# A fused two-block transformer layer on one core: the order of side work and the engine of each copy are read from two tables in the source instead of worked out while the program is built

## The chip, the core and the metric

The kernel runs on one core of a Trainium2 chip. A core has five engines that run their own instruction streams in order and meet at semaphores: TensorE (PE in the profile; its weight loads are listed apart as PEld), VectorE (DVE), ScalarE (ACT), GpSimd (POOL) and SyncE (SP), which here only issues DMAs. The metric is device microseconds of one execution: 865.17, the median of three (864.73 to 866.28).

## What is computed

The reference runs 256 tokens of width 1024, with 16 tokens put in front in the first block, through two blocks in fp32:

```python
# block 1
u = rmsnorm(h, g_pre_mix);  q, k, v, xr, yr = split(u @ w_in)
attn = sliding_window_attention_with_sinks(q, k, v, sinks)   # 8 heads of 64
hr   = rg_lru(causal_depthwise_conv(xr), w_a, b_a, w_x, b_x, lam)
mix  = concat([attn, gelu(yr) * hr]) @ w_out
h = h + rmsnorm(mix, g_post_mix)
h = h + rmsnorm(square(relu(rmsnorm(h, g_pre_ffn) @ w_ff1)) @ w_ff2, g_post_ffn)
# block 2 (after the 16 front tokens are cut off)
u = rms_norm(h, ln_pre_mix);  q_a, k_a, v_a, qkv_b, z_b, b_b, a_b, gate_a, gate_b = split(u @ w_in)
y_a = moba_attention(rope(q_a), rope(k_a), v_a)              # 8 heads of 128
y_b = rms_norm(gated_delta_rule(silu(conv(qkv_b)), decay(a_b), sigmoid(b_b))) * silu(z_b)
merged = sigmoid(gate_a) * (y_a @ w_proj_a) + sigmoid(gate_b) * (y_b @ w_proj_b)
h = h + rms_norm(merged @ w_out, ln_post_mix)
f = rms_norm(h, ln_pre_ffn)
h = h + rms_norm((silu(f @ w_ffn_gate) * (f @ w_ffn_up)) @ w_ffn_down, ln_post_ffn)
h = h + sigmoid(h @ w_ple_gate) * rms_norm(p @ w_ple, ln_ple)
```

## The kernel before

**Products.** Every large product is made in three passes on TensorE, because both factors are split into a hi and a lo part: `mm3` (line 192) issues hi x hi, hi x lo and lo x hi into one PSUM bank. The weights come as 258 tiles of 128x1024 fp32. A tile is loaded by one DMA into `raw` (4 buffers) and split in two halves of 512 columns by `hilo` (line 207): `copy` writes the hi half (`whi`), a VectorE subtraction writes the lo half (`wlo`). Nine pairs of `whi` and `wlo` are held. Activations are split in the same way where they are made (`uT`, `hm`, `mixT`, `yaT`, `mgT`).

**Main work and side work.** `run` (line 327) goes through a list of jobs, each a weight tile or two and its products. Between products a job calls `tick` (line 305). All that isn't a weight product stands in side streams, Python generators started by `side`: the attention of four head pairs (`attn`, line 718), the recurrence gates (`lru_gates`, `rec`), the layer boundaries (`chain_norm`, line 497), and in block 2 the gates, the MoBA attention (`moba2`), the convolved q, k, v (`qkv_post`, line 1086) and the gated delta rule of four head pairs (`gdn`, line 1146). A stream yields the tiles that it needs next. An engine runs its instructions in the order in which the program emits them, so `tick` sets the order on all engines.

**What sets the order.** While the program is built, every call of an engine goes through the class `Timed` (line 101 on), so all instructions of the profile carry its line, L111. It adds an estimated duration to a `Clock` of that engine. `tick` advances a stream when its tiles would be done by TensorE's estimated time, and `prefetch` (line 274) prepares half a weight when one of the next two weights lacks it, or when the estimates of ScalarE, VectorE and the DMA's arrival lie less than `AHEAD` past TensorE's:

```python
on_dve = start_of("dve", src) + (DCP if src.tensor.name in clk.bank else DHI)
if on_dve < start_of("act", src):
    dve.tensor_copy(dst, src)
else:
    act.activation(dst, src, AF.Copy)
...
while s in sides and clk.of(*s[0]) + HOP <= clk.now["pe"] + (LEAD if isinstance(s[0], Soon) else SLACK):
...
    pos["prep"] < pos["use"] + URGENT or
    max(clk.now["act"], clk.now["dve"], arrival()) < clk.now["pe"] + AHEAD):
```

**Names that come up later.** In block 1: `s_m` and `s_r` are the softmax maxima and sums, the copies `g<-ps` of 128x512 in `q_post` bring two query pairs out of PSUM, `mixT` is the split input of w_out, its last rows made by `rec` (line 821) from a GpSimd product. At a layer boundary `m` is the product with the gain, `ms` the mean square, raised to the power -1/2 by GpSimd, `h` the residual and `u` the normed tile, which TensorE transposes into `uT`. In block 2: `gm` is a GpSimd product of gates and a mask, which a TensorE product with `mgt` (line 1111) turns into the decay of a head pair. `A` in `gdn` is the scaled product of k with itself, multiplied with a mask on GpSimd; `cmp` is the sum over it, which goes through a scratch tensor `sc` in memory to 32 rows of `w`, on which GpSimd runs a recurrence of 28 small operations (`tmp`, `g`); `sk`, `rk`, `bk`, `nk` are scalars of the rows of k.

Of the kernel before, what the change touches and what calls it, by code (L numbers as in the profile page):

```python
# [53 lines left out]
SAME = dict(act=0.1, dve=0.12, pool=0.1, pe=0.0, dma=0.0)  # L54


class Clock:


    def __init__(self):  # L60
        self.now = dict.fromkeys(("act", "dve", "pool", "pe", "dma"), 0.0)
        self.done, self.read, self.by = {}, {}, {}
        self.bank, self.user = {}, {}

    def of(self, *tiles):
        return max((self.done.get(t.tensor.name, 0.0) for t in tiles), default=0.0)

    def step(self, eng, cost, outs, ins):
        t = self.now[eng]
        for n in ins:  # L70
            t = max(t, self.done.get(n, 0.0) + (HOP if self.by.get(n) != eng else SAME[eng]))
            if n in self.bank:
                t = max(t, self.bank[n] if self.user.get(n) != eng else 0.0)
        for n in outs:
            if n in self.bank:
                t = max(t, self.read.get(n, 0.0), self.done.get(n, 0.0) if self.by.get(n) != eng else 0.0)
        end = t + cost
        self.now[eng] = end - 2.0 if eng == "dma" else end
        for n in ins:
            self.read[n] = max(self.read.get(n, 0.0), end)  # L80
            if n in self.bank:
                self.bank[n], self.user[n] = end, eng
        for n in outs:
            self.done[n], self.by[n] = end, eng


class Soon(tuple):
    pass


def parts_of(x):

    n = x.tensor.name
    if not n.startswith("uT"):
        return [n]
    dims = [d[1] for d in x.ap[1:]]
    (k, c), m = divmod(x.offset, TM), dims[0] if len(dims) > 1 else 1
    return [f"{n}.{i}.{j}" for i in range(k // 4, (k + m - 1) // 4 + 1) for j in range(c // P, (c + dims[-1] - 1) // P + 1)]


class Timed:


    def __init__(self, clock, eng, name):
        self.clock, self.eng, self.name = clock, eng, name

    def __getattr__(self, op):
        call = getattr(self.eng, op)

        def f(*args, **kw):  # L110
            r = call(*args, **kw)  # L111
            aps = [(k, x) for k, x in list(enumerate(args)) + list(kw.items()) if hasattr(x, "tensor")]
            outs = [n for k, x in aps if k in (0, "out", "accum_out") for n in parts_of(x)]
            ins = [n for k, x in aps if k not in (0, "out", "accum_out") for n in parts_of(x)]
            o = args[0] if args else kw["out"]
            n = o.free_size()
            if "dma" in op:
                self.clock.step("dma", 2.0 + 3.1e-6 * n * o.partition_size() * 4, outs, ins)
                return r
            if self.name == "pe":  # L120
                if op == "transpose":
                    cost = 0.11
                elif kw["rhs"].dtype == F32R:
                    cost = max(0.104, 0.422e-3 * n)
                else:
                    cost = 1.69e-3 * max(n, kw["lhsT"].free_size())
            elif self.name == "act":
                extra = sum(hasattr(kw.get(k), "tensor") for k in ("accum_out", "scale", "bias"))
                cost = (0.051 if ins[0] in self.clock.bank else 0.093) + 0.833e-3 * n + 0.093 * extra
            elif self.name == "dve":  # L130
                m = max(x.free_size() for k, x in aps)
                cost = 0.07 + (0.52e-3 if op == "tensor_copy" and ins[0] not in self.clock.bank else 1.04e-3) * m
            elif kw.get("op") == ALU.pow:
                cost = 0.3 + 0.165 * n
            elif op == "tensor_scalar":
                cost = 0.175 + 3.33e-3 * n + 0.09 * (len(aps) - 2)
            else:
                cost = 0.15 + 2.1e-3 * n
            self.clock.step(self.name, cost, outs, ins)
            return r  # L140
        return f
# [3 lines left out]
def griffin_then_moba_gdn_kernel(ctx: ExitStack, tc, a, out):  # L145
    nc = tc.nc
    clk = Clock()
    act, dve, pool, pe, dma = (Timed(clk, e, n) for e, n in (
        (nc.scalar, "act"), (nc.vector, "dve"), (nc.gpsimd, "pool"), (nc.tensor, "pe"), (nc.sync, "dma")))
# [104 lines left out]
    def prep():  # L254
        i = pos["prep"]
        if not half:
            assert i < pos["free"] + NW
# [21 lines left out]

    def weight(j):  # L280
        i = pos["base"] + j
        pos["use"] = max(pos["use"], i + 1)
        while pos["prep"] <= i:
            prep()
        return wts[i]

    def free(j):
        pos["free"] = pos["base"] + j
        for i in [i for i in wts if i < pos["free"]]:
            del wts[i]  # L290
# [1222 lines left out]
```

## Time and profile before

| what | value |
|---|---|
| median of three runs | 865.17 us (864.73 to 866.28) |
| the profiled execution | 865.83 us, span 864.0 |
| TensorE busy | 848.0 us, 98% |
| VectorE busy | 620.3 us, 72% |
| ScalarE busy | 449.9 us, 52% |
| GpSimd busy | 160.0 us, 19% |
| DMA | 147.18 MB, 170 GB/s on the mean |

The span runs from the first to the last instruction that the profiler saw; 1.83 us of the profiled execution lie around it. Busy time counts instructions, so an engine can be busy and still run slower than it could (TensorE at a lower clock, VectorE beside GpSimd). A timeline row gives the start, the duration of all the instructions merged in it, the engine, the operation, output and inputs, the count, and in square brackets the idle time just before with what ended it.

### The profile page before, as it was taken

How to read it: one execution, taken by the hardware profiler on the slowest of the kernel's cores; microseconds unless marked ns; L12 is line 12 of the kernel's file. 1: busy time of each engine (PE TensorE's matmuls, PEld its weight loads, DVE VectorE, ACT ScalarE, POOL GpSimd, SP SyncE). 2: the span in 40 equal slices, each digit the busy share in tenths (PEclk: the TensorE clock that was granted, in tenths of full speed). 3: DMA queues.
4: the chain of work that ended last, by engine and by line, in shares of the span. 5: the costliest groups of instructions: out<-in, count | busy, mean ns of one | idle time of the engine just before them, and what ended most of it. 6: DMA issues, size and time to landing. Idle time of an engine off the chain costs nothing.

```text
span 864.0 us, 15454 instructions
## 1 busy us (share of the span) xinstructions
PE 848.0 (98%) x5905; PEld 777.2 (90%) x5905; DVE 620.3 (72%) x1135; ACT 449.9 (52%) x1004; POOL 160.0 (19%) x248
## 2 busy tenths in 40 slices
PE   9999999999999999999999999999999999999997
PEld 7988679999999789999989999999977999999987
DVE  6996887555555558988788899777857756655562
ACT  6756666554445454446644473455536544544441
POOL 3411100000000005220363568401300001000001
PEclk9999999999999999999999999999999999999999
DMA  7645537766566246234661345445636768565611
GB/s 260 235 122 178 196 109 262 242 193 195 194 186 186 68 131 235 84 116 145 210 213 50 102 153 184 153 144 181 196 129 183 236 211 277 184 197 179 192 50 50
DMA packets 47772, 147.18 MB, mean 170 GB/s; under 512 B 9281, under 2 KB 10561, under 8 KB 47698
## 3 DMA queue, kind: packets, MB, share of 16 engines
q1 hardware_dynamic: 47554, 146.13, 52.6%
q8 instruction: 46, 0.75, 0.4%
q14 instruction: 28, 0.23, 0.1%
q10 hardware_dynamic: 144, 0.07, 0.0%
HBM read 143.82 MB, written 2.36 MB: 169 GB/s over the span
## 4 chain that ended last, share of the span: by engine, by line
PE 80%; DVE 7%; POOL 5%; DMA 3%; ACT 3%; issue 2%; SPq 0%; POOLq 0%; ACTq 0%; DVEq 0%
PE ps L111 80%; POOL g L111 3%; DVE g L111 2%; DVE wlo L111 2%; POOL tmp L111 2%; ACT g L111 1%; ACT whi L111 1%; DVE s_m L111 1%; DMA raw<-in_w1in 1%; DMA raw<-in_ff1t 1%; DMA xmt<-in_meta 1%; DVE whi L111 0%; DMA gain<-in_rows 0%; DVE u L111 0%; POOL aq L111 0%
## 5 line engine op out<-in xcount | busy, mean ns | idle before, releaser
L111 PE MATMUL ps<-uT,whi 128*128 128x256 f32 (+1 forms) x2272 | 418.1, 285 | 0.0
L111 DVE TENSOR_TENSOR wlo<-raw,whi 128x512 fp32r<-128x512 f32 x513 | 349.4, 724 | 85.8 <-ACT whi L111 83.2
L111 PEld LDWEIGHTS ps<-uT,whi 128*128 128x128 f32 x2272 | 351.9, 189 | 4.5 <-issue 0.8
L111 ACT ACTIVATE whi<-raw 128x512 fp32r<-128x512 f32 x485 | 275.3, 622 | 101.3 <-issue 65.2
L111 PE MATMUL ps<-uT,wlo 128*128 128x256 f32 (+1 forms) x1136 | 319.5, 281 | 0.0
L111 PEld LDWEIGHTS ps<-uT,wlo 128*128 128x128 f32 x1136 | 215.4, 190 | 0.0
L111 PE MATMUL ps<-whi,hm 128*128 128x512 f32 x432 | 138.8, 393 | 0.0
L111 ACT ACTIVATE g<-ps 128x512 f32<-128x512 f32 (+4 forms) x104 | 51.4, 508 | 124.0 <-PE ps L111 122.0
L111 PEld LDWEIGHTS ps<-whi,hm 128*128 128x128 f32 x432 | 81.3, 188 | 17.6
L111 PE MATMUL ps<-wlo,hm 128*128 128x512 f32 x216 | 85.0, 394 | 0.0
L111 PE MATMUL ps<-whi,uT 128*128 128x512 f32 (+1 forms) x256 | 75.8, 376 | 1.0 <-ACT uT L111 0.7
L111 PE MATMUL ps<-g 128*128 128x128 f32 (+9 forms) x560 | 73.0, 278 | 3.1 <-ACT g L111 1.9
L111 POOL TENSOR_TENSOR ms<-ms,mhalf 128x1 f32<-128x1 f32 (+1 forms) x19 | 11.7, 615 | 347.4 <-DVE ms L111 347.3
L111 PEld LDWEIGHTS ps<-g 128*128 128x128 f32 (+5 forms) x560 | 62.6, 176 | 9.3 <-issue 3.1
L111 PEld LDWEIGHTS ps<-whi,uT 128*128 128x128 f32 x256 | 46.3, 191 | 12.2 <-DVE uT L111 2.4
L111 POOL TENSOR_TENSOR g<-g 128x512 f32<-128x512 f32 (+1 forms) x20 | 31.5, 1580 | 113.2 <-DVE g L111 91.9
L111 PEld LDWEIGHTS ps<-wlo,hm 128*128 128x128 f32 x216 | 40.6, 188 | 8.3
L111 PE MATMUL ps<-wlo,uT 128*128 128x512 f32 (+1 forms) x128 | 47.5, 371 | 0.0
L111 DVE SCALAR_TENSOR_TENSOR g<-ps,vec,g 128x255 f32<-128x255 f32 (+5 forms) x84 | 35.0, 475 | 2.7 <-ACT g L111 2.4
L111 ACT ACTIVATE junk<-ps 128x128 bf16<-128x128 f32 (+1 forms) x48 | 17.9, 382 | 30.1 <-PE ps L111 30.0
L111 ACT ACTIVATE hm<-g 128x512 fp32r<-128x512 f32 x23 | 14.5, 632 | 32.5 <-DVE g L111 32.5
L111 DVE SCALAR_TENSOR_TENSOR g<-g,ps 128x512 f32<-128x512 f32 x23 | 15.7, 681 | 17.3 <-ACT g L111 14.3
(166 smaller groups left out, 870.1 us busy)
## 6 DMA issues: line engine op xcount, KB each, us to landing
raw<-in_ff SPq DMA_DIRECT2D x60, 512.0 KB, 4.4
raw<-in_w2qkv SPq DMA_DIRECT2D x24, 512.0 KB, 3.8
raw<-in_ffdown SPq DMA_DIRECT2D x22, 512.0 KB, 4.4
raw<-in_ffg SPq DMA_DIRECT2D x18, 512.0 KB, 4.4
raw<-in_ffu SPq DMA_DIRECT2D x18, 512.0 KB, 4.0
raw<-in_w1in SPq DMA_DIRECT2D x14, 512.0 KB, 4.2
raw<-in_w1out SPq DMA_DIRECT2D x8, 512.0 KB, 3.5
gain<-in_rows SPq DMA_DIRECT2D x16, 256.0 KB, 5.7
```

What stands on the lines that cost most here:

```text
L111: r = call(*args, **kw)
```

## The change

The classes `Clock` and `Timed`, the functions that read them (`start_of`, `arrival`, `prefetch`, `free`, `idle`) and their constants go. Two strings take their place. `ORDER_OF_WORK` says, for the n-th call of `tick`, what is done there: `p` prepares half a weight, a name advances a side stream once, `name*2` twice. `VECTOR_COPIES` lists by stream and number the copies that VectorE makes; ScalarE makes the others. Where the kernel looped on `idle` until something was ready (`when`, `tok_split`) it now calls `tick` once. The boundary chains are started inside `tick`'s round.

```diff
-    def start_of(eng, src):
-        return max(clk.now[eng], clk.of(src))
-
     def copy(dst, src):
-        on_dve = start_of("dve", src) + (DCP if src.tensor.name in clk.bank else DHI)
-        if on_dve < start_of("act", src):
+        n = stream[-1]
+        i = copied[n] = copied.get(n, -1) + 1
+        if i in on_vector.get(n, ()):
             dve.tensor_copy(dst, src)
         else:
             act.activation(dst, src, AF.Copy)
...
+ORDER_OF_WORK = """
+1:p,spill,p,p,p,p,p,p 9:spill 17:p,p 23:p,p,p,p,p,p 24:lru0,lru1,lru1,lru1 28:p,p,p,p,lru3,lru2,lru3,lru3,p 59:p,vtok
...
+VECTOR_COPIES = """
+m:0,3,8,9,14,15,17,18,21,22,26,28,29,35,37,38 spill:1 p3:1 p5:1 p8:1 p10:0 p12:0 p14:0 attn0:0,1 p17:0 attn2:0,2
...
-    def prefetch():
-        while pos["prep"] < min(len(flat), pos["free"] + NW) and (
-                pos["prep"] < pos["use"] + URGENT or
-                max(clk.now["act"], clk.now["dve"], arrival()) < clk.now["pe"] + AHEAD):
-            prep()
...
-    def tick(weights=True):
+    def tick():
         for fn in posts[:]:
             posts.remove(fn)
             fn()
-        for s in sides[:]:
-            while s in sides and clk.of(*s[0]) + HOP <= clk.now["pe"] + (LEAD if isinstance(s[0], Soon) else SLACK):
-                if not advance(s):
-                    break
-        if weights:
-            prefetch()
...
+        pos["step"] += 1
+        for x in plan.get(pos["step"], ()):
+            if x == "p":
+                prep()
+                continue
+            key, _, n = x.partition("*")
+            for _ in range(int(n or 1)):
+                advance(key)
...
     def when(u):
-        while u() is None:
-            idle()
+        tick()
         return u()
```

The program has the same 5611 matrix products of the same shapes, the same GpSimd operations and the same 316 DMA issues. ScalarE has 670 activations instead of 883, VectorE 248 copies instead of 35. Of the 213 copies that change engine, 167 are hi halves of weights (VectorE 31 before, 198 now). Between the transposition of the first pair's k in `gdn` and the product with `mgt` of the second pair TensorE has 290 products before and 326 now.

First place: VectorE in block 2, from the preparation of the first pair's A (the row that reads `bk`) to the reduction that starts the recurrence. Before:

```order
L111 TENSOR_TENSOR wlo_4603<-raw_4457,whi_4602 128x512
L111 TENSOR_TENSOR wlo_4639<-raw_4501,whi_4638 128x512
L111 TENSOR_TENSOR bk_4581<-rk_4580 128x4
L111 SCALAR_TENSOR_TENSOR nk_4582<-sk_4578,rk_4580 128x4
L111 TENSOR_TENSOR bk_4581<-bk_4581,beta_100 128x4
L111 TENSOR_TENSOR wlo_4639<-raw_4501,whi_4638 128x512
L111 TENSOR_TENSOR wlo_4662<-raw_4533,whi_4661 128x512
L111 SCALAR_TENSOR_TENSOR g_4674<-ps_4675,bk_4581,g_4393 128x128 x4
L111 TENSOR_TENSOR wlo_4662<-raw_4533,whi_4661 128x512
L111 TENSOR_TENSOR wlo_4699<-raw_4570,whi_4698 128x512 x2
L111 TENSOR_TENSOR wlo_4719<-raw_4630,whi_4718 128x512 x2
L111 TENSOR_REDUCE cmp_4738<-g_4686 128x64
```

And now, from the row that makes A (L1110); `sk`, the product of k and q, `bk`, `nk` and `bk` stand directly ahead of it:

```order
L1110 SCALAR_TENSOR_TENSOR g_4629<-ps_4630,bk_4601,g_4498 128x128 x4
L178 TENSOR_TENSOR wlo_4644<-raw_4399,whi_4643 128x512
L172 CAST whi_4643<-raw_4399 128x512
L178 TENSOR_TENSOR wlo_4644<-raw_4399,whi_4643 128x512
L172 CAST whi_4651<-raw_4515 128x512
L178 TENSOR_TENSOR wlo_4652<-raw_4515,whi_4651 128x512
L172 CAST whi_4651<-raw_4515 128x512
L178 TENSOR_TENSOR wlo_4652<-raw_4515,whi_4651 128x512
L178 TENSOR_TENSOR wlo_4699<-raw_4523,whi_4698 128x512
L172 CAST whi_4698<-raw_4523 128x512
L178 TENSOR_TENSOR wlo_4699<-raw_4523,whi_4698 128x512
L1118 TENSOR_REDUCE cmp_4706<-g_4641 128x64
```

The four lo subtracts ahead of A are gone (between `sk` and `bk` stands now only the product of k and q with the decay), and between A and the reduction five subtracts became six subtracts and four copies of hi halves.

Second place: VectorE at the first layer boundary, between the two token tiles of block 1's mixer. Before:

```order
L111 TENSOR_TENSOR m<-ps,gain 128x512
L111 SCALAR_TENSOR_TENSOR ms<-ss 128x1
L111 SCALAR_TENSOR_TENSOR h_77<-m,ms,h_77 128x512 x2
L111 TENSOR_TENSOR m<-ps,gain 128x512
L111 SCALAR_TENSOR_TENSOR ms<-ss 128x1
L111 TENSOR_TENSOR wlo<-raw,whi 128x512
L111 SCALAR_TENSOR_TENSOR u<-h_77,ms,gain 128x512 x2
L111 TENSOR_TENSOR m<-ps,gain 128x512
```

And now:

```order
L444 TENSOR_TENSOR m<-ps,gain 128x512
L304 SCALAR_TENSOR_TENSOR ms<-ss 128x1
L450 SCALAR_TENSOR_TENSOR h_77<-m,ms,h_77 128x512 x2
L304 SCALAR_TENSOR_TENSOR ms<-ss 128x1
L172 CAST whi<-raw 128x512
L178 TENSOR_TENSOR wlo<-raw,whi 128x512
L461 SCALAR_TENSOR_TENSOR u<-h_77,ms,gain 128x512 x2
L444 TENSOR_TENSOR m<-ps,gain 128x512 x2
```

The second tile's `m` moved from ahead of the second `ms` to behind `u`, and a hi half was added ahead of `u`.

Third place: VectorE where the two branches of `rec` make the last rows of `mixT`. Before:

```order
L111 TENSOR_TENSOR mixT<-ps,mixT 128x256
L111 TENSOR_SCALAR g<-g 128x512
L111 TENSOR_TENSOR mixT<-ps,mixT 128x256 x2
L111 SCALAR_TENSOR_TENSOR g<-g 128x512 x2
L111 TENSOR_TENSOR wlo<-raw,whi 128x512 x4
L111 TENSOR_TENSOR mixT<-g,mixT 128x512 x2
L111 TENSOR_TENSOR wlo<-raw,whi 128x512 x10
```

And now:

```order
L764 SCALAR_TENSOR_TENSOR g<-g 128x512
L178 TENSOR_TENSOR mixT<-ps,mixT 128x256
L172 COPY g<-ps 16x256
L178 TENSOR_TENSOR wlo<-raw,whi 128x512
L172 CAST whi<-raw 128x512
L178 TENSOR_TENSOR wlo<-raw,whi 128x512 x3
L764 SCALAR_TENSOR_TENSOR g<-g 128x512
L178 TENSOR_TENSOR mixT<-g,mixT 128x512
L172 CAST mixT<-ps 128x256
L178 TENSOR_TENSOR mixT<-ps,mixT 128x256
L178 TENSOR_TENSOR wlo<-raw,whi 128x512 x2
L178 TENSOR_TENSOR mixT<-g,mixT 128x512
```

The two products of the branches, which GpSimd waits for, and the two subtracts into `mixT` behind them were next to each other; now weights and the attention's last `mixT` rows stand between the first branch and the second.

## Rows read from the trace of the kernel before

**Rows 1.** The page's first part: busy time, share and instructions of each engine

```profile
PE 848.0 (98%) x5905; PEld 777.2 (90%) x5905; DVE 620.3 (72%) x1135; ACT 449.9 (52%) x1004; POOL 160.0 (19%) x248
```

**Rows 2.** Waits of TensorE: engine, line, whom for: us, times, longest

```profile
PE ps L111 <- POOL gm L111: 2.0, 2, 1.3
PE ps L111 <- ACT g L111: 1.9, 1, 1.9
PE ps L111 <- DVE u L111: 1.5, 1, 1.5
...
PE ps L111 <- ACT uT L111: 0.7, 3, 0.2
PE ps L111 <- DVE mixT L111: 0.7, 1, 0.7
PE ps L111 <- DVE wlo L111: 0.7, 2, 0.5
PE ps L111 <- POOL g L111: 0.6, 1, 0.6
PE ps L111 <- DVE g L111: 0.5, 2, 0.3
```

**Rows 3.** Windows: length, busy PE, PEld, DVE, ACT, POOL, granted clock, DMA share, GB/s

```profile
50.00:60.00 10.00, 8.07 (x72) 7.65 (x70) 9.62 (x29) 4.39 (x18) 0.00 (x0) 1.00 0.23 67
90.00:100.00 10.00, 8.61 (x28) 5.59 (x27) 9.50 (x14) 5.65 (x10) 1.81 (x2) 0.83 0.55 188
110.00:120.00 10.00, 8.68 (x33) 6.45 (x34) 8.08 (x15) 5.67 (x13) 1.44 (x3) 0.83 0.13 41
340.00:400.00 60.00, 59.41 (x489) 58.51 (x488) 54.85 (x102) 26.87 (x71) 13.02 (x9) 1.00 0.37 116
430.00:440.00 10.00, 10.00 (x86) 10.00 (x86) 6.97 (x13) 5.64 (x11) 8.29 (x22) 1.00 0.85 307
440.00:460.00 20.00, 18.04 (x135) 17.42 (x134) 16.21 (x33) 7.50 (x22) 7.11 (x11) 0.91 0.36 110
```

**Rows 4.** Groups by form: count | busy us, mean ns | idle before

```profile
L111 DVE TENSOR_TENSOR wlo<-raw,whi 128x512 fp32r<-128x512 f32 x513 | 349.4, 724 | 85.8 <-ACT whi L111 83.2
...
L111 DVE CAST whi<-raw 128x512 fp32r<-128x512 f32 x31 | 15.5, 500 | 0.5 <-PE ps L111 0.4
...
L111 ACT ACTIVATE whi<-raw 128x512 fp32r<-128x512 f32 x485 | 275.3, 622 | 101.3 <-issue 65.2 <-PE ps L111 13.8 <-DMA raw<-in_w2qkv 4.4
```

**Rows 5.** Timelines, 413 to 449: start, us, engine, operation (GpSimd, VectorE, TensorE)

```profile
413.96 1.67 POOL L111 TENSOR_TENSOR g<-g,cst 128x512 f32<-128x512 f32 x1
418.83 4.02 POOL L111 TENSOR_TENSOR g<-g,cst 128x512 f32<-128x512 f32 x1 [3.20 <-DVE g L111]
...
418.61 3.09 DVE L111 TENSOR_TENSOR wlo<-raw,whi 128x512 fp32r<-128x512 f32 x5
...
444.81 2.44 POOL L111 TENSOR_TENSOR gm<-glr,cst 128x512 fp32r<-128x512 f32 x2
...
445.08 1.27 DVE L111 CAST whi<-raw 128x512 fp32r<-128x512 f32 x1
...
446.12 0.50 PE L111 MATMUL ps<-gm,mgt 128*128 128x512 f32 x1 [1.27 <-POOL gm L111]
```

**Rows 6.** Timelines, 87 to 112: the recurrent branches and the first boundary

```profile
88.43 3.38 POOL L111 TENSOR_TENSOR g<-g 128x512 f32<-128x512 f32 x2 [5.15 <-DVE g L111]
...
88.87 4.70 DVE L111 TENSOR_TENSOR wlo<-raw,whi 128x512 fp32r<-128x512 f32 x4
...
108.57 0.69 DVE L111 TENSOR_TENSOR m<-ps,gain 128x512 f32<-128x512 f32 x1 [1.42 <-ACT junk L111]
...
111.27 0.96 PE L111 MATMUL ps<-ident,u 128*128 128x128 f32 x5 [1.52 <-DVE u L111]
```

**Rows 7.** Timeline, 57 to 58: ScalarE ahead of the second query copy

```profile
57.50 0.21 ACT L111 ACTIVATE s_r<-s_m 128x4 f32<-128x4 f32 x1 [0.85 <-DVE s_m L111]
...
57.61 0.61 ACT L111 ACTIVATE whi<-raw 128x512 fp32r<-128x512 f32 x1
```

More of the change, by code (lines that the diff above doesn't have):

```diff
@@ L53 @@
 ORDER = "0 ga 1 2 3 pa z gb"
[L54 to L84, printed above, removed]
@@ L87 @@
[L87 to L141, printed above, removed]
@@ L254, in prep, with prep_ @@
     def prep():
+        stream.append(f"p{pos['prep']}")
+        prep_()
+        stream.pop()
+    def prep_():
         i = pos["prep"]
         if not half:
-            assert i < pos["free"] + NW
             while pos["dma"] <= i:
                 weight_dma()
-            half[:] = [wp.tile([P, D], F32R, tag=n, name=n) for n in ("whi", "wlo")]
+            half[:] = wts[i] = [wp.tile([P, D], F32R, tag=n, name=n) for n in ("whi", "wlo")]
             split(i, 0, *[x[:, 0:512] for x in [raws[i]] + half])
@@ L269, in prep, with advance, side @@
             weight_dma()
-    def arrival():
-        return clk.of(raws[pos["prep"]]) if pos["prep"] in raws else 1e9
-    def prefetch():
-        while pos["prep"] < min(len(flat), pos["free"] + NW) and (
-                pos["prep"] < pos["use"] + URGENT or
-                max(clk.now["act"], clk.now["dve"], arrival()) < clk.now["pe"] + AHEAD):
-            prep()
-    def weight(j):
[L281 to L290, printed above, removed]
-    def advance(s):
-        y = next(s[1], END)
-        if y is END:
-            sides.remove(s)
-        else:
-            s[0] = () if y is None else y if isinstance(y, (tuple, list)) else (y,)
-        return y is not END and y is not None
-    def side(g, first=False):
-        s = [(), g]
-        sides.insert(0 if first else len(sides), s)
-        advance(s)
-    def tick(weights=True):
+    def weight(j):
+        return wts[pos["base"] + j]
+    def advance(key):
+        s = sides[key]
+        assert s[1] is None or s[1]()
+        stream.append(key)
+        y = next(s[0], END)
+        stream.pop()
+        s[1] = y if callable(y) else None
+    def side(g, key):
+        sides[key] = [g, None]
+        advance(key)
+    def tick():
         for fn in posts[:]:
@@ L395, in fn @@
                 st["ps"] = pt()
-            w = kview(weight(0), KD)
             for k in range(KD):
-                mm3(st["ps"][:, m * T:(m + 1) * T], [x[k] for x in w], when(lambda: rhs(k)), k == 0, k == KD - 1)
+                r = when(lambda: rhs(k))
+                mm3(st["ps"][:, m * T:(m + 1) * T], [x[:, blk(k)] for x in weight(0)], r, k == 0, k == KD - 1)
                 if k % 2:
@@ L440, in fn @@
             for t in range(2):
-                while not ready[t]:
-                    idle()
+                tick()
+                assert ready[t]
                 if t == 1:
@@ L457, in when @@
     def when(u):
[L458 to L459 removed]
+        tick()
         return u()
@@ L468, in fn @@
                 acc[:] = [[pt(), pt()] for t in range(2)]
-            w = kview(weight(0), 2)
             for t in range(2):
                 for j in range(2):
-                    ko1(acc, w, when(u), j, t, first, False)
+                    x = when(u)
+                    ko1(acc, kview(weight(0), 2), x, j, t, first, False)
                     tick()
@@ L487, in fn @@
                     for i in range(n):
-                        ko1(acc, kview(weight(i), 2), when(us[i]), j, t, False, i == n - 1)
-                        if t and j:
-                            free(i + 1)
+                        x = when(us[i])
+                        ko1(acc, kview(weight(i), 2), x, j, t, False, i == n - 1)
+                        if i == n - 1:
+                            fin.add((t, j))
+                            if j == 0:
+                                side(chain(acc, t, fin), f"norm{b}{t}")
                         tick()
-                    fin.add((t, j))
-                    if j == 0:
-                        side(chain(acc, t, fin), True)
         job(list(srcs), fn)
@@ L501, in chain @@
             for j in range(2):
-                while (t, j) not in fin:
-                    yield
-                yield Soon([acc[t][j]])
+                yield lambda: (t, j) in fin
+                yield [acc[t][j]]
                 m.append(gt(nm="m"))
@@ L743, in attn @@
         copy(pT_[1], ps[1])
-        while "vtok" not in S1:
-            yield
+        yield lambda: "vtok" in S1
         vtok = S1["vtok"]
@@ L828, in rec @@
         dve.scalar_tensor_tensor(y, in0=y2, scalar=1.0, in1=y, op0=ADD, op1=MUL)
-        while "done" not in S1["lru"][c]:
-            yield
+        yield lambda: "done" in S1["lru"][c]
         yield S1["lru"][c]["m2"]
@@ L1046, in post @@
             if n == "k":
[L1047 removed]
+                side(moba2(S2["qk"][p], S2["v"][p // 2], p % 2, S2["ya"], p), f"moba{p}")
         return post
[L1049 removed]
+    tok_split([(a["w2v"][i], v_post(i)) for i in range(2)], lambda: side(gdn_gates(), "gates"))
     for p in range(4):
```

134 lines of the change are left out of this document (83 added, 51 removed).

## The prediction, as it was put on record

> **What bounds the kernel now.** I read the page's first part, then the waits of TensorE, then windows for the clock, then timelines at the waits found. The page shows TensorE busy for 848.0 of 864.0 us [rows 1]. The change leaves all 5611 matrix products, the weight loads and the 316 DMA issues as they are, so only what TensorE lacks can be won: waits, and time at the lower clock. The waits behind the kernel's start are eight, 2.0 + 1.9 + 1.5 + 0.7 + 0.7 + 0.7 + 0.6 + 0.5 = 8.6 us [rows 2]. The windows show the granted clock at 0.83 in 90 to 100, 0.83 in 110 to 120, and 0.91 in 440 to 460 [rows 3]. These are mixtures of the two levels, 2.4 and 1.2 GHz; what each fall lost is (1 - 0.83) x 10 = 1.7 us, again 1.7, and (1 - 0.91) x 20 = 1.8, together 5.2 us. The falls lie where TensorE waits for wlo and mixT, for u (until 111.27, [rows 6]) and for gm (until 446.12, [rows 5]); the wait of 1.9 us for a query copy, in 50 to 60, was followed by none (1.00 there, [rows 3]). So at most 8.6 + 5.2 = 13.8 us can go, 1.6%.
>
> **What the change moves.** Two tables fix the order and the engine of each copy. 213 copies go from ScalarE to VectorE; 167 of them are the hi halves of weights. One costs 622 ns on ScalarE and 500 ns on VectorE; the lo subtract that follows on VectorE costs 724 [rows 4]. That is about 167 x 0.5 = 84 us more VectorE work beside 620.3 of 864 [rows 1]. It is off the path as long as weights are prepared ahead (nine are held), and VectorE no longer waits for ScalarE's hi half. So the sum is made at TensorE's waits.
>
> *gm and its clock, 2.0 + 1.8.* At 446.12 - 1.27 = 444.85 TensorE wants gm, which GpSimd makes only behind the recurrence of head pair 0; both halves are done at 444.81 + 2.44 = 447.25, 2.4 us late [rows 5]. The recurrence starts late too: its masked product took 4.02 us on GpSimd from 418.83, while five lo subtracts ran on VectorE from 418.61; the same form just before it took 1.67 [rows 5]. GpSimd's own order is the same after the change. On TensorE there are 290 products between the transposition of that pair's k and the product that reads gm, now 326: 36 more, at 10 us / 86 = 0.116 us each [rows 3], is 4.2 us more room. Ahead of the recurrence the VectorE queue loses four lo subtracts between the gate scalars and A (first place of the order): 4 x 0.72 = 2.9 us, of which I count half, as GpSimd's power for rk lies beside them. Against that, ten rows instead of five stand between A and the reduction: 6 x 0.72 + 4 x 0.5 = 6.3 us; if they hold GpSimd's product as the five did, it starts up to 6.3 - 3.1 = 3.2 later. Balance: 4.2 + 1.5 - 2.4 - 3.2 = +0.1 at worst, +3.3 at best. The wait goes in both cases; I take -3.8, bounds -3.8 and 0. The Trainium skill, "SBUF — State Buffer", section "Who interferes with whom", says that a vector instruction with two SBUF inputs, or a copy or cast in a fast mode, and a GpSimd instruction that reads SBUF shut each other out for a whole instruction, whichever starts first. By it the moved casts would hold the product as the subtracts do, and this is the +0.1 end. The trace agrees for a cast: 1.27 us beside gm [rows 5], against a mean of 0.50.
>
> *u and its clock, 1.5 + 1.7.* At the first layer boundary VectorE's m waited 1.42 us for ScalarE's junk, up to 108.57 [rows 6], and stood ahead of the second ms, hence of GpSimd's power and of u. In the new order ms follows h directly and m comes behind u; in return a cast, 0.5, stands ahead of u (second place). 1.42 - 0.5 = 0.9 to 1.4 of 1.5 goes. If the rest is short the fall may go with it, but it is not sure: -2.4, bounds -0.9 and -3.2.
>
> *wlo and mixT with their clock, 0.7 + 0.7 + 1.7.* GpSimd's two products from 88.43 met VectorE's four lo subtracts, which took 4.70 us instead of 4 x 0.72 = 2.9 [rows 6]; behind these came the two mixT subtracts and a weight. The new order parts the two recurrent branches, so that each mixT is made when its product is, and puts one to three lo subtracts between (third place). ScalarE also loses nine copies of weights in this stage. I take -2.4, three quarters of it; bounds 0 and -3.1.
>
> *The query copy, 1.9.* On ScalarE the copy of the second query pair stood behind the exponential of s_m (57.50, after 0.85 of waiting) and a hi half of 0.61 from 57.61 [rows 7]. The half now stands behind it: -0.6. The exponential's wait for VectorE stays (bounds 0 and -1.9).
>
> *The rest, uT 0.7, g 0.6 and 0.5.* Copies of transposed tiles are shared between the two engines now, and side streams are taken earlier. Half: -0.9, bounds 0 and -1.8.
>
> *What is added.* (1) In 50 to 60 VectorE is busy 9.62 of 10 [rows 3], and it now makes the first pair's query copy directly ahead of its scores, and later a mixT copy; one lo subtract ahead of such a copy is 0.72. I take +1.0, bounds 0 and 1.9 (as the wait on ScalarE now). (2) In the delta rule five copies out of PSUM, and in the MoBA attention seven, go to VectorE, whose queue is fuller; a product waits for each. Half a lo subtract each is 12 x 0.36 = 4.3; about a third I take to be uncovered by other products: +1.4, bounds 0 and 4.3.
>
> Sum: -3.8 - 2.4 - 2.4 - 0.6 - 0.9 + 1.0 + 1.4 = -7.7. The profiled run took 865.83 us (span 864.0 and 1.83 around it), so 858.1. The median of the runs shown, 865.17, is 0.66 lower: 857.5.
>
> **Rivals.** *VectorE becomes the bound where copies stand densest (slower).* In 340 to 400 it is busy 54.85 of 60 [rows 3]. Among the 500 matrix products of about this stretch (the 1950th to the 2450th) the order puts 11 more copies and 6 more lo subtracts: 11 x 0.5 + 6 x 0.72 = 9.8, hence 64.7 of 60: 4.7 us too much. If each of the copies also meets GpSimd (busy 13.02 there, and all through the recurrences) at 1.27 instead of 0.50, that is 8.5 more: 13.2. It decides when the lead of prepared weights is used up; below 4.7 nothing shows. 865.17 - 7.7 + 13.2 = 870.7. For it: the one cast at gm. Against it: VectorE gains the idle time before lo subtracts, 85.8 us over the kernel [rows 4], and six subtracts moved in from neighbours mean a longer lead. Chance 0.12.
>
> *Only gm goes.* VectorE is the bound of the first 120 us, and its waits there only change names: -3.8, half of the rest (-0.5) and half of what is added (+1.2) are -3.1: 862.1. For it: 9.62 of 10 busy in 50 to 60 [rows 3]. Against: the wait for u came from an order, not from load. Chance 0.17.
>
> *Gains eaten by new tight places.* What is added costs its upper ends, 1.9 + 4.3 = 6.2, and the terms other than gm bring half, -3.1: -3.8 - 3.1 + 6.2 = -0.7, or 864.5. For it: copies that now stand directly ahead of their products, in the fuller of the two queues. Against: on ScalarE they stood behind work too. Chance 0.11.
>
> *Nearly all goes.* A list that removes all eight waits and the three falls: 865.17 - 13.8 = 851.4. For it: every wait here has work beside it that could stand elsewhere. Against: the three waits for uT, 0.2 each [rows 2], come from chains with nothing between. Chance 0.15.
>
> **How the numbers follow.** The forecast has 0.45; the five add up to 1. A measurement of this kernel tells 0.2%, 1.7 us, from no change. Faster by that (below 863.4) are the forecast with 0.43, the ceiling with 0.15, "only gm" with 0.14 and the eaten gains with 0.03: 0.75. No change: 0.02 of the forecast, 0.03 of "only gm", 0.06 of the eaten gains, 0.02 of the overloaded VectorE: 0.13. Slower (above 866.9): 0.10 of the overload and 0.02 of the eaten gains: 0.12. The range reaches down past the ceiling by two small stalls that no wait row names, 849.5, and up to 866.0, which takes in all but the slower rival; the forecast's own range, with the bounds of its terms partly cancelling, is 853 to 861.
>
> **What would show it.** In the profile after: no gm among TensorE's waits, and the clock at 1.00 in the window that holds the gm products; the wait for u below 0.6; mixT and wlo below 0.5 together; VectorE busy near 725 us (the 46 other copies at some 0.5 each on top of the 84) and ScalarE near 325; the waits that are left named for copies of g on VectorE. The forecast is wrong if the clock still falls in two or more places, if TensorE waits for wlo by more than 2 us in 340 to 430, or if GpSimd's recurrences end later against the products that need them.

## The result, and the profile after

The changed kernel takes 853.73 us (median of four, 853.2 to 854.28) against 865.66 us for the kernel before (median of four, 864.73 to 866.28): a ratio of 0.9863, 95% interval 0.9846 to 0.9880, or 11.9 us. Measured again beside other kernels on another occasion it was 853.21 against 865.07, 0.9875 (0.9854 to 0.9895). The prediction was 857.5 with a range of 849.5 to 866.0: the sign and the range held, the size was 7.7 for 11.9. The time lies nearer to 851.4, the rival "nearly all goes", which had a chance of 0.15.

The page's first part for the changed kernel, which answers to [rows 1]: busy time, share of the span (851.6 us), instructions.

```profile
PE 839.2 (99%) x5905; PEld 772.7 (91%) x5905; DVE 695.8 (82%) x1348; ACT 338.8 (40%) x791; POOL 153.6 (18%) x248
```

VectorE has 75.5 us more and ScalarE 111.1 less; the prediction named 725 and 325 us, and VectorE's copies were cheaper than assumed (437 ns for a hi half instead of 500, below). The waits of TensorE in the changed kernel, which answer to [rows 2] (engine, waiting line, whom for: us, times, longest; the lines now are the real ones, L1041 is in the convolution of q, k, v, L1159 in the delta rule, L496 the attention's exponential, L581 the start):

```profile
PE ps L324 <- DVE u L581: 1.5, 2, 1.2
PE ps L183 <- DVE g L1041: 1.1, 1, 1.1
...
PE ps L674 <- ACT g L496: 1.0, 1, 1.0
PE ps L161 <- DVE g L1159: 1.0, 1, 1.0
PE ps L161 <- ACT g L174: 0.6, 1, 0.6
PE ps L161 <- ACT uT L174: 0.4, 1, 0.4
PE ps L1163 <- DVE g L1191: 0.3, 1, 0.3
PE ps L324 <- DVE u L461: 0.2, 1, 0.2
PE ps L161 <- DVE uT L178: 0.2, 1, 0.2
```

gm, wlo, mixT and GpSimd's g are gone, u at the boundary (L461) is 0.2 instead of 1.5. Behind the start the waits left are for ScalarE in the attention (1.0 and 0.6), for uT at the first boundary (0.4 and 0.2) and, in block 2, for three rows of VectorE: a product of the convolution (L1041, 1.1), and a transposition and a subtraction of the delta rule (L1159, 1.0; L1191, 0.3). Windows of the changed kernel, answering to [rows 3] (length, busy time of PE, PEld, DVE, ACT, POOL, granted clock, DMA share, GB/s):

```profile
80.00:100.00 20.00, 20.00 (x102) 15.72 (x101) 16.15 (x30) 10.23 (x22) 3.53 (x3) 1.00 0.64 209
100.00:120.00 20.00, 19.38 (x99) 15.64 (x98) 17.11 (x31) 11.68 (x26) 1.77 (x3) 1.00 0.27 82
350.00:400.00 50.00, 50.00 (x418) 49.71 (x417) 47.08 (x96) 22.91 (x61) 6.34 (x5) 1.00 0.45 148
430.00:440.00 10.00, 10.00 (x84) 9.90 (x84) 9.67 (x20) 3.79 (x8) 8.94 (x16) 1.00 0.44 125
440.00:460.00 20.00, 18.99 (x163) 18.66 (x161) 19.72 (x47) 9.33 (x26) 6.42 (x5) 1.00 0.36 108
```

The granted clock is 1.00 in each: none of the three falls is left. From 350 to 400, the place of the slower rival, VectorE is busy 47.08 of 50 and TensorE misses nothing. From 440 to 460 VectorE is full and TensorE waits 1.0. The groups of [rows 4] now (count | busy us, mean ns | idle before):

```profile
L178 DVE TENSOR_TENSOR wlo<-raw,whi 128x512 fp32r<-128x512 f32 x513 | 346.0, 709 | 24.5 <-ACT whi L174 15.5
L172 DVE CAST whi<-raw 128x512 fp32r<-128x512 f32 x198 | 86.6, 437 | 0.4 <-DMA raw<-in_ffu 0.3
...
L174 ACT ACTIVATE whi<-raw 128x512 fp32r<-128x512 f32 x318 | 183.2, 624 | 144.5 <-DMA raw<-in_ff 35.3 <-DMA raw<-in_ffg 19.8 <-DMA raw<-in_w2qkv 15.9
```

VectorE's idle time ahead of lo subtracts fell from 85.8 to 24.5 us, and that bought nothing by itself: in e1 below it is 39.6 us, and e1 is faster still. Timelines at the two places of [rows 5] and [rows 6] (start, us, engine, operation):

```profile
408.75 1.60 POOL L1115 TENSOR_TENSOR g<-g,cst 128x512 f32<-128x512 f32 x1 [1.60 <-DVE g L1110]
...
408.52 0.68 DVE L178 TENSOR_TENSOR wlo<-raw,whi 128x512 fp32r<-128x512 f32 x1
409.12 1.52 DVE L172 CAST whi<-raw 128x512 fp32r<-128x512 f32 x1
...
411.28 0.42 DVE L172 CAST whi<-raw 128x512 fp32r<-128x512 f32 x1
...
437.43 2.05 POOL L1048 TENSOR_TENSOR gm<-glr,cst 128x512 fp32r<-128x512 f32 x2
...
439.57 0.63 PE L161 MATMUL ps<-gm,mgt 128*128 128x512 f32 x2
...
81.58 1.28 POOL L767 TENSOR_TENSOR g<-g 128x512 f32<-128x512 f32 x1 [3.19 <-DVE g L764]
87.55 1.68 POOL L767 TENSOR_TENSOR g<-g 128x512 f32<-128x512 f32 x1 [4.69 <-DVE g L764]
...
101.46 0.16 DVE L304 SCALAR_TENSOR_TENSOR ms<-ss 128x1 f32<-128x1 f32 x1 [0.85 <-ACT junk L300]
```

gm is done at 437.43 + 2.05 = 439.48 and read at 439.57: the room that the order made is 0.1 us. In three other executions with the same rows there, e11, e5 and e6, it is 0.1, 0.4 and nothing, without a wait. GpSimd's masked product took 1.60 this time and it was VectorE's copy that was held, 1.52 against a mean of 0.44.

**Where the time went.** For each form of product (tiles and shapes) I took the median distance from its start to the next product's start, in the trace of before; TensorE's lag over a stretch is the time it took less the sum of these distances. The stretches are cut by amounts of such work (the first column; the clock time is up to 30 us later). Each column is one profiled execution; e1 to e11 are the experiments of the next section. Lag in us:

| work, us | what lies there | before | after | gm alone (e8) | hi on VectorE (e2) | hi on ScalarE (e1) | mixed (e7) | three undone (e10) |
|---|---|---|---|---|---|---|---|---|
| 0-40 | start | 2.7 | 0.9 | 1.5 | 5.7 | 0.9 | 0.5 | 1.2 |
| 40-75 | attention | 4.6 | 4.4 | 5.9 | 6.2 | 5.0 | 4.4 | 4.4 |
| 75-95 | recurrent branches, mixT | 4.3 | 0.5 | 3.6 | 5.2 | 0.5 | 0.5 | 1.8 |
| 95-100 | first boundary, u | 3.9 | 1.2 | 4.4 | 2.3 | 1.2 | 1.2 | 2.4 |
| 100-415 | to the delta rule | 3.6 | 2.0 | 4.4 | 10.7 | 1.8 | 2.0 | 1.8 |
| 415-430 | gm | 4.1 | 0.1 | 0.1 | 6.6 | 0.1 | 0.1 | 5.0 |
| 430-580 | delta rule | 4.6 | 7.5 | 5.4 | 12.1 | 5.2 | 5.1 | 6.3 |
| 580-828 | the rest | 1.9 | 0.9 | 1.8 | 2.0 | 1.3 | 0.8 | 0.6 |
| sum | | 29.7 | 17.5 | 27.1 | 50.6 | 16.0 | 14.5 | 23.5 |

The sums differ by 12.2 between before and after, the spans by 864.0 - 851.6 = 12.4.

### The profile page after: what moved, and what is told of

Same layout as the page of the kernel before. It is cut to its first block, busy times and chain, and to the rows that moved or that the text cites. A ratio compares the mean times of both kernels' runs of the same rounds, so it can differ in the third digit from the quotient of the medians.

```text
span 851.6 us, 15382 instructions
## 1 busy us (share of the span) xinstructions
PE 839.2 (99%) x5905; PEld 772.7 (91%) x5905; DVE 695.8 (82%) x1348; ACT 338.8 (40%) x791; POOL 153.6 (18%) x248
## 4 chain that ended last, share of the span: by engine, by line
PE 76%; DVE 15%; DMA 3%; ACT 2%; issue 2%; POOL 2%; SPq 0%; DVEq 0%; ACTq 0%; POOLq 0%
PE ps L161 74%; DVE wlo L178 4%; DVE g L1032 2%; DVE whi L172 1%; PE ps L324 1%; DVE s_m L490 1%; DMA raw<-in_w2qkv 1%; PE ps L183 1%; DVE g L488 1%; POOL tmp L1134 1%; POOL g L1136 1%; DVE g L1041 1%; ACT g L496 1%; DMA raw<-in_w2ga 1%; ACT whi L174 1%
## 5 line engine op out<-in xcount | busy, mean ns | idle before, releaser
L178 DVE TENSOR_TENSOR wlo<-raw,whi 128x512 fp32r<-128x512 f32 x513 | 346.0, 709 | 24.5 <-ACT whi L174 15.5
L174 ACT ACTIVATE whi<-raw 128x512 fp32r<-128x512 f32 x318 | 183.2, 624 | 144.5 <-DMA raw<-in_ff 35.3
L172 DVE CAST whi<-raw 128x512 fp32r<-128x512 f32 x198 | 86.6, 437 | 0.4 <-DMA raw<-in_ffu 0.3
L174 ACT ACTIVATE g<-ps 128x256 f32<-128x256 f32 (+4 forms) x37 | 15.7, 434 | 41.9 <-PE ps L161 20.5
L874 ACT ACTIVATE g<-ps 128x512 f32<-128x512 f32 x14 | 8.3, 594 | 59.6 <-PE ps L161 59.6
L1134 POOL TENSOR_TENSOR tmp<-g 32x14 f32<-32x14 f32 (+6 forms) x56 | 24.7, 442 | 29.6 <-DMA g<-sc 25.8
L1032 DVE SCALAR_TENSOR_TENSOR g<-ps,vec,g 128x255 f32<-128x255 f32 (+2 forms) x72 | 29.1, 472 | 0.2 <-ACT g L1028 0.2
L875 DVE TENSOR_TENSOR g<-g 128x512 f32<-128x512 f32 x14 | 9.6, 689 | 22.2 <-ACT g L874 22.2
```

The lines of the kernel that those rows point to most:

```text
L178: (eng or dve).tensor_tensor(lo, src, hi.bitcast(F32), op=SUB)
L875: dve.tensor_tensor(r, r, r, op=MUL)
L1032: dve.scalar_tensor_tensor(xc[:, o + s:o + T], in0=ps[:, o:o + T - s], scalar=V("conv2", col[m] - s), in1=xc[:, o + s:o + T], op0=MUL, op1 ...
L1134: pool.tensor_tensor(tmp, w[:, 0:j, j:j + 1].to_broadcast([32, j, 15 - j]), w[:, j:j + 1, j + 1:].to_broadcast([32, j, 15 - j]), op=MUL)
```

## The experiments

**e1: the order without the moved weights.** All entries `p0` to `p257` leave `VECTOR_COPIES`, so the 198 hi halves go to ScalarE; the 50 other copies stay.

```diff
 VECTOR_COPIES = """
-m:0,3,8,... spill:1 p3:1 p5:1 p8:1 p10:0 ... p257:0,1 norm41:0
+m:0,3,8,... spill:1 attn0:0,1 attn2:0,2 attn3:1,3 ... norm41:0
 """
```

> The order of the changed kernel, with all 198 hi halves of weights back on ScalarE (the 50 other copies stay where the table puts them). Theory A, the order makes the gain: ScalarE goes from 339 to about 339 + 198 x 0.62 = 462 us busy, VectorE from 696 to 609, TensorE's waits stay within 2 us of the changed kernel's, 852 to 857. Theory B, moving the hi halves to VectorE makes the gain, because a lo subtract no longer waits for another engine: at least half of the 11.9 us comes back, 860 to 866.

Measured: 852.23 us (852.12 to 852.47), ratio 0.9854 (0.9842 to 0.9867). Its busy times:

```profile
PE 839.7 (99%) x5905; PEld 772.6 (91%) x5905; DVE 617.3 (73%) x1150; ACT 442.1 (52%) x989; POOL 152.9 (18%) x248
```

Theory B falls: with the engines loaded almost as before the whole gain is there, and 1.0 to 1.5 us more. What e1 leaves changed is the order and the engine of the other copies (50 on VectorE instead of 4); the two were not parted.

**e2: the moved weights without the order.** The kernel before, its planner deciding as ever, but each hi half is issued on the engine of the new table.

```diff
     def split(i, j, src, hi, lo):
-        hilo(src, hi, lo, pool if i < 2 and (i, j) != (0, 1) else dve)
+        hilo(src, hi, lo, pool if i < 2 and (i, j) != (0, 1) else dve, (i, j) in HI_ON_VECTOR)
```

> The kernel before, instruction for instruction in its own order on TensorE, GpSimd and SyncE, but each hi half of a weight on the engine that the new table names (198 on VectorE instead of 31). Theory A, order: no gain, the gm wait and the three clock falls stay, 862 to 872 (more VectorE work in an order that was laid out for less). Theory B, engine: half or more of the gain, 854 to 860.

Measured: 887.8 us (885.89 to 889.31), ratio 1.0265 (1.0252 to 1.0279), worse than either theory said. The longest waits of TensorE in it:

```profile
PE ps L131 <- DVE g L131: 6.6, 9, 3.0
PE ps L131 <- POOL gm L131: 4.6, 2, 4.1
PE ps L131 <- DVE uT L131: 2.7, 2, 2.5
PE ps L131 <- DVE wlo L131: 2.4, 5, 1.5
```

The lag grows in nearly all stretches. So the move of the hi halves costs 22.8 us in the old order and 1.0 to 1.5 in the new. The cover that the prediction took for granted is thus no property of VectorE's free time (it has 689 busy of 885 here). That it comes from where the new order puts the preparation of weights is my reading; no run moves that alone.

**e3 and e8: gm alone, in the old order.** In e3 the planner is told that gm of the second pair is done 4.5 us later, so it places the product later; in e8 only the two rows of the product and the exponential behind them are issued later, and the planner's estimates stay as they were. From e3:

```diff
+                    if p == 1:
+                        for g in gm:
+                            clk.done[g.tensor.name] += LATER
                     yield gm
```

From e8, where `emit` issues the two rows:

```diff
+                    if p == 1:
+                        def emit():
...
+                        held.append([Timed.products + LATER, emit])
```

> The kernel before with one thing moved: TensorE's product that reads gm of the second pair stands 42 products later (2838 instead of 2796 ahead of it), so 42 x 0.116 = 4.9 us later. If the gm term of the prediction is right, 2.0 us of waits and the clock fall after them go: -3.8, or 861.4 to 862.5. If a wait of this length costs only itself, -2.0 and the fall stays: 863.5. If the room is used up by something behind it (the decay is late next): no change, 865.5.

Measured for e3: 866.55 us (864.25 to 868.92), ratio 1.0016 (1.0004 to 1.0028). The lag in 415 to 430 is 0.1, as hoped, but TensorE then waits 3.7 us for g on VectorE in 440 to 570, where before it waited 0.2.

> The kernel before with only the gm product and the exponential behind it moved, by 42 products, and every other row of every engine in its place (in the earlier run with gm later, other rows had moved too, and waits for g on VectorE of 3.7 us took back what gm had given, 4.1 at its place). If those waits came from the other rows: -3.8, or 861.2. If they come from the decay that is now late: 864 to 866.

Measured for e8: 862.7 us (861.49 to 864.12), ratio 0.9963 (0.9950 to 0.9976), 3.4 us less than the kernel before beside it. The windows of e8 at the place:

```profile
430.00:440.00 10.00, 10.00 (x87) 10.00 (x86) 7.12 (x15) 5.24 (x10) 7.99 (x22) 1.00 0.87 311
440.00:460.00 20.00, 20.00 (x169) 19.81 (x168) 19.67 (x38) 9.03 (x26) 9.12 (x14) 1.00 0.35 111
```

TensorE misses nothing and the clock stays: the gm term is shown, at 3.4 of the 3.8 predicted. With the decay as late as in e3 no loss follows, so what e3 lost came from the other rows that the planner moved when one estimate changed (some 160 on TensorE and 60 on VectorE).

**e4: gm put back in the new order.** One entry of the table moves, which moves the product 30 products ahead.

```diff
-1383:p,gdn0 ... 1400:qkv10,qkv12,qkv12,gdn1
+1383:p,gdn0,qkv10 ... 1400:qkv12,qkv12,gdn1
```

> The changed kernel with the same product put back: 30 products earlier (2814 instead of 2844 ahead of it), 3.5 us; nothing else moves on VectorE, GpSimd and SyncE, and one copy on ScalarE. In the changed kernel the product stands 0.1 us behind gm's end, so it must now wait about 3.3 us. If a fall of the clock follows such a wait: 3.3 + 1.7 = 5.0, or 858.7. If the wait costs only itself: 857.0.

Measured: 856.83 us (856.2 to 857.08), 3.1 above the changed kernel. TensorE and the windows in e4:

```profile
438.22 0.52 PE L161 MATMUL ps<-gm,mgt 128*128 128x512 f32 x1 [2.59 <-POOL gm L1048]
439.23 0.80 PE L161 MATMUL ps<-gm,mgt 128*128 128x512 f32 x1 [0.49 <-POOL gm L1048]
...
430.00:440.00 10.00, 6.92 (x51) 6.29 (x50) 9.57 (x22) 2.51 (x5) 8.72 (x15) 0.93 0.37 113
440.00:450.00 10.00, 10.00 (x80) 10.00 (x79) 8.76 (x21) 5.13 (x17) 0.00 (x0) 0.90 0.33 107
```

The wait of 3.1 us is back, and a fall of the clock with it (0.93 and 0.90, 0.7 + 1.0 = 1.7 us). At the place 4.9 us are lost; the time is only 3.1 to 3.7 longer, since the delta rule behind it then lags less (7.0 instead of 7.5) and the start of this execution was 0.5 shorter.

**e5: the recurrent branches together again.**

```diff
-147:p,rec0,rec0*2,rec1,attn2*2,attn3 149:p,p,p,p 154:rec1,rec1*2,rec0 156:attn3*2 163:p 169:p,rec1 179:p
+147:p,rec1,attn2*2,attn3 154:rec0,rec1,rec0*2,rec1*2 156:attn3*2,p,p,p,p 163:rec0,rec1,p 169:p 179:p
```

> The changed kernel with the two recurrent branches put together again as before (on VectorE the two g products side by side, then four lo subtracts, then the two mixT subtracts; GpSimd's two products side by side). If the order of these rows is what removed the mixT and wlo waits and the fall near 93: 1.4 us of waits come back, with the fall 3.1 to 3.8, so 856.8 to 857.5. If it was something else, such as nine copies less on ScalarE in this stage: 853.7 within 1.

Measured: 855.33 us (853.24 to 859.45). TensorE in the profiled execution (853.24):

```profile
91.80 0.73 PE L161 MATMUL ps<-whi,mixT 128*128 128x512 f32 x2 [1.02 <-DVE mixT L178]
```

The mixT wait is back, 1.0, without wlo and in this execution without a fall. Two of the six executions, 858.94 and 859.45, had a granted clock of 0.995 where the others had 0.999 to 1.0. So the order of these rows brings the mixT wait. That the falls of the two executions lie in this stretch is not shown, as they were not profiled. The rest of the 3.9 us that the stretch gained isn't taken back: it lags 1.8 here, against 4.3 before and 0.5 in the changed kernel.

**e6: m ahead of ms again.**

```diff
-193:p,p,p,p,norm10*2,p,p,norm10*2,norm10,norm10,norm10,p 195:norm10 203:norm11*2,norm11*2,norm11,norm10,norm10
+193:p,p,p,p,norm10*2,p,p,norm10*2,norm10,norm10,norm11*2,norm10,p 195:norm10 203:norm11*2,norm11,norm10,norm10
```

> The changed kernel with one VectorE row moved back: the second tile's first m stands ahead of the second ms again (ScalarE's square of the same bank moves with it). If the u term of the prediction is right, the wait for u at the first boundary grows by 0.9 to 1.4 us, and by 1.7 more if the clock falls after it: 854.8 to 856.8. If m costs nothing there: 853.7 within 0.5.

Measured: 854.75 us (853.43 to 856.68). VectorE and TensorE at the boundary in e6:

```profile
102.87 0.69 DVE L444 TENSOR_TENSOR m<-ps,gain 128x512 f32<-128x512 f32 x1 [1.43 <-ACT junk L300]
...
105.51 1.23 PE L324 MATMUL ps<-ident,u 128*128 128x128 f32 x8 [0.73 <-DVE u L461]
```

m waits 1.43 us for ScalarE ahead of ms, as it did before (1.42), and u's wait is 0.9 instead of 0.2: 0.7, with a median 1.0 to 1.5 higher. No fall followed here; the profiled execution, 856.68 and the longest of the four, has one elsewhere (0.83 in 460 to 470), behind a wait of 2.0 us for L1159 of the delta rule. The interval of one such difference is about 1.5 us, so it is the trace that shows this, not the time.

**e10: the three places undone at once** (e4, e5 and e6 in one table), with the changed kernel itself beside it (e11).

> The changed kernel with three places put back at once: gm's product earlier, the two recurrent branches together, m ahead of ms. Singly they cost 3.1, 1.6 and 1.0 us. If the places add up: 859.4. If they make the clock fall more often together than singly (the kernel before has two to four falls in an execution): 861 to 864.

> The changed kernel as it is, beside the two others on the same chip, so that differences of 1 to 3 us are taken against it: 853 to 855. Its clock should stay at 0.999 to 1.0 in every execution, against 0.992 to 0.998 of the kernel before.

Measured: 858.39 us (857.21 to 860.44), and 853.21 (852.9 to 856.27) for the changed kernel. The three places are worth 5.2 us, near the sum of the single ones (5.7). They are less than half of the 11.9. In the trace of e10 the waits are back, 2.8 for gm, 1.6 for u and 1.0 for mixT, but a fall only behind gm (0.83 in 440 to 450; 1.00 from 90 to 120). One execution of the changed kernel in e11, 856.27, had a clock of 0.997, which the expectation had ruled out.

**e7 and e9: a better version.** In e7 the 18 hi halves of the weights 132 to 165 go back to ScalarE; e9 also moves the second attention pair's transpositions from step 103 to 109.

```diff
-p133:0,1 p134:1 p137:1 p141:0 p142:0,1 p143:1 p144:1 p145:1 p149:0 p150:0 p153:0 p158:1 ... p159:1 p161:0 p164:0 p165:1
-103:attn1,p,p,p,p,p 109:attn2
+103:p,p,p,p,p 109:attn1,attn2
```

> The changed kernel with 18 hi halves (of the weights 132 to 165, prepared during the delta rule) back on ScalarE, the other 180 on VectorE. With all 198 back the run gained 1.5 us, and its lag behind TensorE's pure work was 2.1 smaller in just this stretch. If VectorE's load there is what costs: 851.2 to 852.4. If the gain came from elsewhere: 853.7 within 0.5.

> The mixed kernel (18 hi halves of the delta rule on ScalarE) with one more move: the transpositions of the second attention pair's probabilities 12 products later (1.4 us), because TensorE waited 1.0 us there for ScalarE's exponential. If only that wait goes: 1.0 less than the mixed kernel's 851.2, so 849.9 to 850.6. If the copies behind the transpositions are late next: no change, 850.8 to 851.6.

Measured: e7 851.18 us (850.59 to 852.97; eight executions of the changed kernel lie at 852.9 to 856.27), ratio 0.9836 (0.9819 to 0.9852), the fastest here with e9: 850.93 (850.11 to 852.33), ratio 0.9838 (0.9822 to 0.9854). Windows of 430 to 460 and 460 to 520, of e7 and of the changed kernel:

```profile
430.00:460.00 30.00, 30.00 (x257) 29.78 (x256) 29.58 (x67) 13.83 (x35) 14.42 (x18) 1.00 0.40 126
460.00:520.00 60.00, 59.29 (x511) 57.63 (x511) 52.50 (x112) 33.13 (x99) 41.09 (x73) 1.00 0.39 121
```

```profile
430.00:460.00 30.00, 28.99 (x246) 28.56 (x245) 29.39 (x67) 13.12 (x33) 15.36 (x21) 1.00 0.39 114
460.00:520.00 60.00, 58.62 (x502) 56.75 (x501) 56.02 (x118) 28.28 (x89) 38.99 (x71) 1.00 0.41 127
```

From 460 on VectorE has 3.5 us less to do and TensorE misses 0.7 instead of 1.4; from 430 it misses nothing instead of 1.0. In e9 the wait for the exponential is gone and the time is the same within the interval, so something else came late in its place. Its trace lags 1.1 less than e7 in 40 to 75 and 1.3 more in 100 to 415, with new waits for a lo half (0.2, at 382.8) and for VectorE's g of the convolution (0.4, at 399.8); whether the move or this execution brought them was not followed up.

## Why the prediction held, and where its sizes were off

| step of the prediction | predicted | measured by stretch | shown by |
|---|---|---|---|
| gm and its clock | -3.8 | -4.0 | e8 -3.4, e4 +3.1 |
| u and its clock | -2.4 | -2.7 | e6: wait +0.7; e10: +1.4; no fall there |
| wlo, mixT and their clock | -2.4 | -3.9 | e5: wait +1.0, stretch +1.3 |
| query copy, and added (1) | +0.4 | -0.2 | not tried |
| the rest | -0.9 | -2.7 (1.7 up to the delta rule, 1.0 behind it) | not tried |
| added (2), delta rule | +1.4 | +2.9 | e7: -2.4 in the stretch, -2.0 to -2.6 in time |
| the start, not in the sum | 0 | -1.7 | other executions, below |

By stretch the sum of 7.7 had 1.5 too little in wlo and mixT, 1.8 in the rest, 1.7 at the start and 1.1 in the three other terms of the gain; against that the cost in the delta rule was 1.5 too small.

- *gm.* The term held, its pieces only in part. The rows of VectorE that set it, before and in the changed kernel:

```profile
412.46 0.16 DVE L111 TENSOR_SCALAR sk<-sk 128x4 f32<-128x4 f32 x1
...
417.57 1.12 DVE L111 SCALAR_TENSOR_TENSOR g<-ps,bk,g 128x128 f32<-128x128 f32 x4
...
422.88 1.06 DVE L111 TENSOR_REDUCE cmp<-g 128x64 f32<-128x512 f32 x1 [1.19 <-POOL g L111]
```

```profile
404.55 0.16 DVE L1092 TENSOR_SCALAR sk<-sk 128x4 f32<-128x4 f32 x1
...
407.48 1.13 DVE L1110 SCALAR_TENSOR_TENSOR g<-ps,bk,g 128x128 f32<-128x128 f32 x4
...
415.08 1.05 DVE L1118 TENSOR_REDUCE cmp<-g 128x64 f32<-128x512 f32 x1
```

  From `sk` to the end of A it is 2.2 us shorter (predicted 1.5). From there to the reduction it is 2.3 longer (predicted 0 to 3.2), and not because GpSimd's product was held: the reduction stood behind the ten rows in VectorE's own queue. From the reduction to gm's end it is 24.4 both times. So gm is no earlier behind `sk` (34.8 and 34.9 us); what removed the wait is TensorE's longer way from `sk` to the product, by 2.6 us (predicted 4.2) against a delay of 2.4. With 0.1 us left over, that it went whole is in part luck. Of the lock that the Trainium skill describes ("SBUF — State Buffer", "Who interferes with whom") the trace shows the other side: GpSimd's product had started first, at 408.75, and VectorE's copy of 409.12 was shut out (1.52 us), which agrees with the rule (the one that starts first shuts the other out).
- *u.* The wait went as told: ms no longer stands behind m. Its price of 1.42 us is seen again in e6. That the fall in 110 to 120 hung on this wait is not shown: in e10 the wait is back (1.6) and no fall follows it.
- *wlo and mixT.* The term was mis-sized: three quarters of 3.1 us were taken, and the stretch lost 4.3 and now 0.5. Next to the named waits three products there started 0.36 to 0.37 late without a wait row of their own, two of them while the clock was down; these went too.
- *The query copy.* Its wait of 1.9 is gone, but TensorE now waits 1.0 for the exponential and 0.6 for a copy, both on ScalarE; the cost came there and not on VectorE, where added (1) had it.
- *The rest.* Mis-sized: the two stretches gained 2.7 for 0.9 predicted. The rows of [rows 2] were halved without reading where each comes from. Of 1.5 us of wait rows there (g 0.6, uT 0.7 and another 0.2 on VectorE) 0.2 are left; the other half of the 2.7 is lag that no wait row names. Which edits did it was not tried.
- *Added (2).* Half the size, and another mechanism. The term priced copies out of PSUM that products wait for; the waits left there are for no moved copy (L1041, L1159, L1191), and sending back 18 hi halves, with the PSUM copies left on VectorE, takes 2.4 of the 2.9 out of the stretch (e7). So most of the cost was in the hi halves, which the prediction had called off the path.
- *"It is off the path as long as weights are prepared ahead."* Nearly true of the new order, at 1.0 to 1.5 us (e1), and false of the old one (e2). The step took the cover from nine buffers and from VectorE's idle time. e2 has both and lost 22.8 us.
- *The slower rival* fell: 47.08 of 50 busy in its stretch and no wait. It is what e2 shows, though, with the old order.
- *The start.* About 1.1 of the 1.7 us were no part of the change. The products `ps<-xg,warm`, in the profiled executions of before and of the changed kernel (duration in ns, least, median and most):

```profile
L111 PE MATMUL ps<-xg,warm x4: 1061/1061/1191, 5.6 to 8.3; 128*128 128x512 f32 x4
```

```profile
L161 PE MATMUL ps<-xg,warm x4: 592/592/667, 4.9 to 6.2; 128*128 128x512 f32 x4
```

  The same rows at 592 stand in e3, which starts with the order of before, and at 1061 in e6, which starts with that of the changed kernel. So the execution decides this, not the order. Over the first 40 us of work e3 and e8 lag 1.5.
- *The falls.* All three went from the profile, as hoped, but a fall is no fixed price. In 40 executions of the kernel before the mean granted clock was 0.992 to 0.998, mean 0.9953; in eight of the changed kernel 0.997 to 1.0. The ten at 0.998 took 864.2 us on the mean, the six at 0.992 took 865.9: 0.006 of 864 is 5.2 us of clock, and the time differs by 1.7. So, as an estimate from these two groups, about a third of a fall's price stays; by it the three falls are worth 1.7 us of time and not 5.2. At gm e8 points to more: it gained 3.4, of which the wait is 2.0.

Of 11.9 us, 5.2 are tied to three places of the order (e10). The remaining 6.7 lie in the stretches that the table shows and were not taken apart. In the traces of before and of e10 4.0 of them lie in 75 to 100 of the work, where before has two falls and e10 has none.

## What to carry to other kernels

When one change moves both the order and the engine of work, run each half alone: here the order, with the copies other than hi halves, gave all of the gain, and the move of the hi halves cost 1.0 to 1.5 us, or 22.8 without the order. A wait that is read from a row, with its queue and the room behind it counted in instructions, can be sized well even where the pieces err (gm: 3.8 predicted, 3.4 in e8); terms that took a half or three quarters without such a reading were off by 1.5 to 1.8 us. A stall that a planner caused was better mended by moving the one row (-3.4 us) than by changing the planner's estimate, which moved some 160 other products and lost the gain (+1.5). An engine with free time on the mean is no cover for added work: look at the stretch where it is full (here 430 to 520), and give back the copies there.

## What the runs showed of the hardware that was not expected

- The clock's falls come and go from execution to execution: eleven of the kernel before on one chip had mean clocks of 0.992 to 0.998. Their places differ too. e8 has the rows of before up to its moved product, beyond 430 us. After the 1.9 us wait near 56 us the profile of before has no fall (1.00 in 50 to 60), e8 has 0.89 in that window; in 90 to 100 the profile of before has a fall (0.83) and e8 has 1.00.

```profile
50.00:60.00 10.00, 8.05 (x63) 7.66 (x63) 9.54 (x31) 5.09 (x20) 0.00 (x0) 0.89 0.30 91
90.00:100.00 10.00, 8.11 (x31) 5.20 (x30) 9.42 (x14) 5.65 (x10) 2.03 (x2) 1.00 0.57 166
```

- At the start the column of the granted clock can mislead: a window of before reads 1.00 while its products take 1061 ns instead of 592.

```profile
4.00:10.00 6.00, 5.20 (x12) 2.87 (x12) 2.14 (x4) 4.23 (x11) 1.31 (x2) 1.00 0.98 339
```

  The trace's records of the clock begin only at 10.6 us in before (10.2 in e6, 3.9 to 6.6 in the others), and time without a record is counted as 1.00. In all 13 traces the products `ps<-xg,warm` behind the first record took 592 to 593 ns (a first one 667 to 668), and those that end ahead of it 1061 (a first one 1190 to 1193). So read the level there from the products.
- A copy of 128x512 on VectorE beside a GpSimd product took 1.52 us, alone 0.42; the GpSimd product, which had started first, took 1.60, within the 1.28 to 1.68 of the other two shown above (against 4.02 when the subtracts were first).
